# Nine more pairs of k tiles by seven products, in the convolution, merge and down blocks of a hybrid decoder layer

## The chip, the core and the metric

The kernel runs on one core of a Trainium2 chip. The metric is the device time of one execution in microseconds, as the median of several runs. TensorE (PE) multiplies, VectorE (DVE) and ScalarE (ACT) prepare its operands and take its results away, SyncE (SP) issues the transfers.

## What is computed

One layer on 256 tokens of width 2048, all in float32. Cut to what matters:

```python
h = rms_norm(x, mix_norm)
cb, cc, cx, q, k, v, g_conv, g_attn = split(h @ w_in)
conv_y = cb * causal_dwconv(cc * cx, conv_mix_w)
branch_conv = conv_y @ w_conv_out
branch_attn = dilated_window_attention(q, k, v) @ w_attn_out
merged = sigmoid(g_conv) * branch_conv + sigmoid(g_attn) * branch_attn
x = x + merged @ w_merge_out
g, u = split(causal_dwconv(rms_norm(x, ffn_norm) @ w_up, ffn_conv_w))
x = x + (silu(g) * u) @ w_down
```

## The kernel before

Every weight is read once, in chunks of 512 KB that SyncE loads into five `raw` buffers, and every chunk is split into a high and a low half: ScalarE rounds it (`whi`), VectorE subtracts (`wlo`, line 140). There are four buffers of each. The activations are held split in the same way, and a product is three matmuls: high by high, high by low, low by high.

The order is written out as a list of steps, one per chunk, and before each step's matmuls the program issues the loads up to eight chunks ahead and the splits up to three (`run_blocks`). A scheduler then puts each engine's instructions in a row, so their places need not be those of the code. Each engine works through its row in order.

The work runs through these blocks: cc, cx and cb (the three convolution inputs, in eight parts, 256 columns a chunk), then the convolution blocks gc, co, gc, co (the gate and the output of the convolution, 1024 columns each), q, k, v and ga (the attention, and its gate), ao (`W_ao`), mo (`W_mo`, the merge, four blocks of 512 columns), then twice eleven parts of ug and uv (the two halves of the up projection) and the down projection dn: two blocks of 1024 columns after the first eleven parts, one of 1024 and two of 512 after the second.

The 1024-column blocks are made by `block_h` and run by `run_h`. They take two k tiles (two chunks) at a time. An ordinary pair is eight products: two halves of tokens by two halves of columns by two tiles. A pair named in `PAIRS` or `DOWN_PAIRS` is a 2 x 2 product of blocks done with seven products on sums of the operands. For that, `split_sums` makes from the two chunks w11, w12, w22, w21 the sums `pq` and `rt` and splits four units, on VectorE:

```python
units = [split_unit(a[:, 1:2])]
nc.vector.tensor_tensor(pq[:, 0], w11, w12, op=ALU.add)
nc.vector.tensor_tensor(pq[:, 1], w12, w22, op=ALU.add)
units.append(split_unit(pq))
units.append(split_unit(b))
nc.vector.tensor_tensor(rt[:, 0], pq[:, 0], w22, op=ALU.add)
nc.vector.tensor_tensor(rt[:, 1], rt[:, 0], w21, op=ALU.add)
units.append(split_unit(rt))
```

A `split_unit` is one `whi` (line 147) and one `wlo` (line 148) and takes one of the four split buffers: the first has 512 columns, the others 1024. `make_forms` makes the four sums of activations that the seven products need, once for each pair. Four of the products gather over all such pairs of a block in `m1`, `m5`, `m6` and `m7` (`m16` holds the first and the third of them in one tile), and after the last such pair `combined` forms four sums of them on VectorE, which are added to the block's accumulators by its closing function.

A block's closing function, on VectorE: after cc, cx, cb, ug and uv a sum of two halves of the accumulator (`fsum`, ScalarE's copy `cba` or `upa` first), products with the norm, and for cx, ug and uv the convolution over three tokens (`dwconv`); after gc four sums; after co eight; after dn four.

Of the kernel before, what the change touches and what calls it, by code (L numbers as in the profile page):

```python
# [15 lines left out]
ALU = mybir.AluOpType  # L16
AX = mybir.AxisListType

P = 128
D = 2048  # L20
S = 256
NT = S // P
KT = D // P
# [7 lines left out]
CW = 512  # L31
# [15 lines left out]

K4_BUFS = 25
K2_BUFS = 16
PAIRS = (2, 4)  # L50
DOWN_PAIRS = (2, 5, 8)
RAW_BUFS = 5
WARM = 8
SPLIT_BUFS = 4
# [14 lines left out]
def hybrid_block(ctx: ExitStack, tc: tile.TileContext, x, x_turned, positions, gains, params, q_norm,  # L69
                 k_norm, w_first, w_rest, out):  # L70

    nc = tc.nc
# [9 lines left out]
    def k4(name, dtype=F32):  # L82
        return kpool.tile([P, 4 * S], dtype, tag="k4", name=name)

    def k2(name, dtype=F32):
        return kpool.tile([P, 2 * S], dtype, tag="k2", name=name, bufs=K2_BUFS)
# [81 lines left out]
    def after(n, fn):  # L168
        cur["n"] += 1
        side.append((cur["chunk"] + n, cur["n"], fn))  # L170
# [39 lines left out]
    def block_h(w, c0, r0, kts, src, forms, pairs, evac, name, **more):  # L210
        b = {"kts": kts, "mode": "H", "src": src, "forms": forms, "pairs": pairs, "evac": evac,
             "name": name, **more}
        blocks.append(b)
        for k in range(kts):
            if k // 2 in pairs:
                strassen[len(steps)] = None if k % 2 == 0 else k // 2
            steps.append((b, k, 1))
            chunks.append((w, r0 + k * P, 1, c0, 2 * CW))
# [68 lines left out]
    def make_forms(z, name, whole=True):  # L287
        t_ = k2(name + "f").rearrange("p (f s) -> p f s", f=4)
        if whole:
            both = k4(name + "F", F32R).rearrange("p (h f s) -> p h f s", h=2, f=4)  # L290
            hi, lo = both[:, 0], both[:, 1]
        else:
            hi, lo = (k2(name + "F", F32R).rearrange("p (f s) -> p f s", f=4) for _ in range(2))
        x11, x12, x21, x22 = (z[:, k, t * P:(t + 1) * P] for t in range(NT) for k in range(2))
        for n, a, b, op in ((0, x22, x21, ALU.subtract), (1, t_[:, 0], x11, ALU.add),
                            (2, x11, x21, ALU.subtract), (3, x12, t_[:, 1], ALU.subtract)):
            nc.vector.tensor_tensor(t_[:, n], a, b, op=op)
        nc.scalar.activation(hi, t_, AF.Copy)
        nc.vector.tensor_tensor(lo, t_, hi.bitcast(F32), op=ALU.subtract)
        return hi, lo  # L300
# [66 lines left out]
    def load_x(t_, c, cw, eng=nc.sync):  # L367
        v = t_.rearrange("p (t n) -> p t n", t=NT)
        eng.dma_start(v, x_v[:, :, c * cw:(c + 1) * cw])
        return v  # L370
# [16 lines left out]
    def row_squares(xs, ssq, c):  # L387
        junk = k2("junk")
        n = xs.shape[2]
        for t in range(NT):  # L390
            nc.scalar.activation(junk[:, :n], xs[:, t, :], AF.Square, accum_out=ssq[:, t, c:c + 1])
# [4 lines left out]
    def transposed(xs, i, gain0, store, name):  # L396
        store[i] = k4(name, F32R)
        pv = parts(store[i])
        tp_ = bank("tp")
        for k in range(2):  # L400
            for t in range(NT):
                done["tp"] = nc.tensor.transpose(tp_[:, k * S + t * P:k * S + (t + 1) * P],
                                                 xs[:, t, k * P:(k + 1) * P], ident)
        for k in range(2):
            g = cols[:, gain0 + 2 * i + k:gain0 + 2 * i + k + 1]
            src = tp_[:, k * S:(k + 1) * S]
            h = nc.scalar.activation(pv[:, k, 0, :], src, AF.Copy, scale=g)
            l = nc.vector.scalar_tensor_tensor(pv[:, k, 1, :], src, g, pv.bitcast(F32)[:, k, 0, :],
                                               op0=ALU.mult, op1=ALU.subtract)
        return h, l  # L410
# [93 lines left out]
    def ev_cb(nb):  # L504
        def evac(ps):
            z = fsum(ps, "cb")

            def gated():
                nc.vector.tensor_tensor(v2(z), v2(z), bc(rb1), op=ALU.mult)
                nc.vector.tensor_tensor(z, z, keep.pop("y"), op=ALU.mult)  # L510
                cy[nb] = split2(z, "conv")
                if nb in PAIRS:
                    cy_forms[nb] = make_forms(v2(z), "conv")
# [232 lines left out]
        return evac  # L746


    mg = [None] * 8

    def ev_attn_out(nb):
        def turned(half):
            i = 2 * nb + half
            mg[i] = k4("mg", F32R)
            pv = parts(mg[i])
            tp_ = bank("tp")
            for k in range(2):
                for t in range(NT):
                    c = (2 * half + k) * P
                    nc.tensor.transpose(tp_[:, k * S + t * P:k * S + (t + 1) * P],  # L760
                                        gattn[nb][t][:, c:c + P], ident)
            tv = tp_.rearrange("p (k s) -> p k s", k=2)
            nc.scalar.activation(pv[:, :, 0, :], tv, AF.Copy)
            nc.vector.tensor_tensor(pv[:, :, 1, :], tv, pv.bitcast(F32)[:, :, 0, :], op=ALU.subtract)

        def evac(ps):
            for t in range(NT):
                nc.vector.tensor_tensor(gattn[nb][t], ps[:, t, :], gattn[nb][t], op=ALU.mult)
                nc.vector.tensor_tensor(gattn[nb][t], gattn[nb][t], m1[nb][t], op=ALU.add)
            for half in range(2):  # L770
                after(1 + half, lambda half=half: turned(half))
        return evac

    x2, H2 = [None] * 4, [None] * 8
    ssq2 = cpool.tile([P, NT, 4], F32, name="ssq2")
    norm2 = {}

    def ev_merge(nb):
        def evac(ps):
            x2[nb] = load_x(k4("x2"), nb, CW)  # L780
            nc.vector.tensor_tensor(x2[nb], ps, x2[nb], op=ALU.add)
            for half in range(2):
                after(half, lambda half=half: transposed(x2[nb][:, :, half * 2 * P:(half + 1) * 2 * P],
                                                         2 * nb + half, 16, H2, "h2"))
            row_squares(x2[nb], ssq2, nb)
            if nb == 3:
                norm2["r"], norm2["rb"] = rms_rows(ssq2, "r2")
                after(3, lambda: rms_bcast(norm2["r"], norm2["rb"]))
        return evac
# [58 lines left out]
    W_in, W_co, W_ao, W_mo, W_up, W_dn = "w_in", "w_conv_out", "w_attn_out", "w_merge_out", "w_up", "w_down"  # L848
# [5 lines left out]
    for nb in range(2):  # L854
        block_h(W_in, COL_GC + nb * 2 * CW, 0, KT, x_src, x_forms, PAIRS, ev_gate_h(gconv, nb), "gc")
        block_h(W_co, nb * 2 * CW, 0, KT, cy_src, cy_forms, PAIRS, ev_conv_out_h(nb), "co")
    for half in range(2):
        for g in range(GROUPS):
            c = (g * SLOTS + half * 4) * HD
            block(W_in, COL_Q + c, 0, KT, "T", x_src, ev_qk(qT, gq, g, "q"), "q")  # L860
            block(W_in, COL_K + c, 0, KT, "T", x_src, ev_qk(kT, gk, g, "k"), "k")
        for g in range(GROUPS):
            c = (g * SLOTS + half * 4) * HD
# [7 lines left out]
    for nb in range(4):  # L871
        block(W_ao, nb * CW, 0, SLOTS, "T", at_src, ev_attn_out(nb), "ao")
    m_src = src_of(mg)
    for nb in range(4):
        block(W_mo, nb * CW, 0, KT, "T", m_src, ev_merge(nb), "mo")
    h_src = src_of(H2)
    for b0, b1 in ((0, NB // 2), (NB // 2, NB)):
# [46 lines left out]
    after(RB_AT, lambda: rms_bcast(r1, rb1))  # L924
    for n, i in enumerate(PAIRS):
        after(56 + 4 * n, behind(lambda i=i: forms_of_x(i)))
# [41 lines left out]
```

## Time and profile before

| what | value |
|---|---|
| median of 3 runs | 1846.84 us (1841.93 to 1851.29) |
| the profiled execution's own time | 1851.43 us |
| its span, first to last instruction | 1849.6 us |
| TensorE busy | 1843.5 us of the span |
| VectorE busy | 1279.6 us |
| ScalarE busy | 950.2 us |
| granted TensorE clock, mean | 1.000 |

The durations of matmuls overlap, so a sum of them is more than the time they take; the time from start to start is what each costs. The same holds to a smaller degree on VectorE: the next instruction can start before the one ahead is shown as ended.

### The profile page before, as it was taken

Reading aid. Unit: us, or ns where it says so; the run is one execution under the profiler, and the core shown is the slowest. Engines: PE = TensorE matmul, PEld = TensorE weight load, DVE = VectorE, ACT = ScalarE, POOL = GpSimd, SP = SyncE. Lnnn points to the kernel's source line nnn. Section 1 sums busy time; section 2 is a strip of 40 time slices with the busy share of each in tenths; the row PEclk is TensorE's granted clock in tenths of the full one; section 3 lists DMA queues with packets and bytes.
Section 4 is the critical chain, followed back from the end, with each engine's and each line's share of the span. In section 5 each row is a group of like instructions: output and inputs, shape, how many; then the busy total and the mean of one; then the engine's idle time right before and its main releaser. Section 6 shows DMA issues by size and latency. Waiting matters only on the chain.

```text
span 1849.6 us, 24483 instructions
## 1 busy us (share of the span) xinstructions
PE 1843.5 (100%) x9305; PEld 1561.4 (84%) x9305; DVE 1279.6 (69%) x1761; ACT 950.2 (51%) x1211; POOL 5.3 (0%) x18
## 2 busy tenths in 40 slices
PE   9999999999999999999999999999999999999999
PEld 8888888888888888888888888888888888888887
DVE  6787667777666474666566656777787867777774
ACT  6555445554555454554544455555554555555542
POOL 0000000000000000000000000000000000000000
PEclk9999999999999999999999999999999999999999
DMA  9555556566555535555535665555556665555563
GB/s 330 187 185 195 191 183 194 193 205 205 180 186 188 194 118 182 182 182 190 185 128 181 205 204 184 191 192 188 190 186 194 203 201 185 185 189 184 182 229 124
DMA packets 100213, 350.56 MB, mean 190 GB/s; under 512 B 11264, under 2 KB 11904, under 8 KB 100096
## 3 DMA queue, kind: packets, MB, share of 16 engines
q1 hardware_dynamic: 99664, 348.59, 57.1%
q8 instruction: 73, 1.20, 0.3%
q10 hardware_dynamic: 432, 0.41, 0.1%
q14 instruction: 44, 0.36, 0.1%
HBM read 346.86 MB, written 2.10 MB: 189 GB/s over the span
## 4 chain that ended last, share of the span: by engine, by line
PE 99%; DMA 0%; ACT 0%; DVE 0%; DVEq 0%; issue 0%; ACTq 0%
PE ps_ug L343 9%; PE ps_uv L343 9%; PE ps_uv L344 5%; PE ps_ug L344 5%; PE ps_cc L343 3%; PE ps_cx L343 3%; PE ps_cb L343 3%; PE ps_dn L235 3%; PE ps_dn L237 3%; PE ps_dn L236 3%; PE ps_k L350 2%; PE ps_q L350 2%; PE ps_v L350 2%; PE ps_k L348 2%; PE ps_q L348 2%; PE ps_k L349 2%
## 5 line engine op out<-in xcount | busy, mean ns | idle before, releaser
L140 DVE TENSOR_TENSOR wlo<-raw,whi 128x1024 fp32r<-128x1024 f32 (+1 forms) x622 | 748.5, 1209 | 436.0 <-ACT whi L139 432.9
L139 ACT ACTIVATE whi<-raw 128x1024 fp32r<-128x1024 f32 (+1 forms) x622 | 650.6, 1048 | 687.9 <-PE ps_ug L343 91.0
L343 PE MATMUL ps_ug<-h,whi 128*128 128x512 f32 x704 | 247.5, 395 | 0.0
L343 PE MATMUL ps_uv<-h,whi 128*128 128x512 f32 x704 | 247.4, 395 | 0.0
L344 PE MATMUL ps_ug<-h,wlo 128*128 128x256 f32 x704 | 197.7, 281 | 0.0
L344 PE MATMUL ps_uv<-h,wlo 128*128 128x256 f32 x704 | 197.4, 280 | 0.0
L343 PEld LDWEIGHTS ps_ug<-h,whi 128*128 128x128 f32 x704 | 132.0, 187 | 31.0
L343 PEld LDWEIGHTS ps_uv<-h,whi 128*128 128x128 f32 x704 | 132.0, 187 | 30.9
L344 PEld LDWEIGHTS ps_ug<-h,wlo 128*128 128x128 f32 x704 | 133.0, 189 | 0.1
L344 PEld LDWEIGHTS ps_uv<-h,wlo 128*128 128x128 f32 x704 | 133.0, 189 | 0.0
L343 PE MATMUL ps_cc<-xT,whi 128*128 128x512 f32 x256 | 92.3, 403 | 1.3 <-DVE xT L905 1.3
L343 PE MATMUL ps_cx<-xT,whi 128*128 128x512 f32 x256 | 91.8, 401 | 0.0
L237 PE MATMUL ps_dn<-whi,act 128*128 128x512 f32 x210 | 81.8, 389 | 0.0
L235 PE MATMUL ps_dn<-whi,act 128*128 128x512 f32 x210 | 81.8, 390 | 0.0
L236 PE MATMUL ps_dn<-wlo,act 128*128 128x512 f32 x210 | 81.7, 389 | 0.0
L343 PE MATMUL ps_cb<-xT,whi 128*128 128x512 f32 x224 | 79.4, 399 | 0.0
L348 PE MATMUL ps_k<-whi,xT 128*128 128x512 f32 x192 | 75.8, 395 | 0.0
L348 PE MATMUL ps_v<-whi,xT 128*128 128x512 f32 x192 | 75.7, 394 | 0.0
L348 PE MATMUL ps_q<-whi,xT 128*128 128x512 f32 x192 | 75.5, 393 | 0.0
L350 PE MATMUL ps_k<-whi,xT 128*128 128x512 f32 x192 | 75.0, 390 | 0.0
L350 PE MATMUL ps_q<-whi,xT 128*128 128x512 f32 x192 | 74.9, 390 | 0.0
L350 PE MATMUL ps_v<-whi,xT 128*128 128x512 f32 x192 | 74.9, 390 | 0.0
(320 smaller groups left out, 3480.2 us busy)
## 6 DMA issues: line engine op xcount, KB each, us to landing
raw<-in_w_rest SPq DMA_DIRECT2D x640, 512.0 KB, 3.4
x<-in_x SPq DMA_DIRECT2D x8, 512.0 KB, 6.8
raw<-in_w_first SPq DMA_DIRECT2D x15, 256.0 KB, 5.4
xt<-in_x_turned SPq DMA_DIRECT2D x8, 256.0 KB, 5.1
out<-x SPq DMA_DIRECT2D x7, 256.0 KB, 5.7
xz<-in_x_turned SPq DMA_DIRECT2D x2, 256.0 KB, 3.6
raw<-in_w_first ACTq DMA_DIRECT2D x1, 256.0 KB, 3.9
taps<-in_params SPq DMA_DIRECT2D x1, 156.0 KB, 5.2
```

Source lines behind the costliest of these rows:

```text
L139: last["act"] = nc.scalar.activation(hi, raw, AF.Copy)
L140: last["dve"] = nc.vector.tensor_tensor(lo, raw, hi.bitcast(F32), op=ALU.subtract)
L235: nc.tensor.matmul(dst, x[0], hi, start=first, stop=False)
L236: nc.tensor.matmul(dst, x[0], lo, start=False, stop=False)
L237: nc.tensor.matmul(dst, x[1], hi, start=False, stop=last)
L343: nc.tensor.matmul(pm, hi[:, j, w_], xs, start=first, stop=False)
L344: done["pe"] = nc.tensor.matmul(pm[:, :S], lo[:, j, w_], xs[:, :S], start=False, stop=last)
L348: nc.tensor.matmul(pm, sh, hi[:, j, :], start=first, stop=False)
L349: nc.tensor.matmul(pm, sh, lo[:, j, :], start=False, stop=False)
L350: nc.tensor.matmul(pm, sl, hi[:, j, :], start=False, stop=last)
```

## The change

`PAIRS` gets a third pair, and all its pairs move: 1, 3, 5 in place of 2, 4 of the eight. `DOWN_PAIRS` gets a fourth, 1, 3, 6, 8 in place of 2, 5, 8 of the eleven. The first two blocks of the merge become one 1024-column block in which pairs 3 and 5 take seven products; its forms are made as the gates are turned, its share of `x` is loaded then, and its sums are added to `x2` when the second pair is done. The rest of the merge stays as it is.

```diff
-PAIRS = (2, 4)
-DOWN_PAIRS = (2, 5, 8)
+PAIRS = (1, 3, 5)
+MERGE_PAIRS = (3, 5)
+DOWN_PAIRS = (1, 3, 6, 8)
...
-    mg = [None] * 8
+    mg, mg_forms = [None] * 8, {}
...
+            if i == MERGE_PAIRS[-1]:
+                for c in range(2):
+                    x2[c] = load_x(k4("x2"), c, CW)
+            if i in MERGE_PAIRS:
+                z = k2("mgz")
+                nc.scalar.copy(z, tp_)
+                mg_forms[i] = make_forms(z.rearrange("p (k s) -> p k s", k=2), "mg", False)
...
+    def merge_sums(sums):
+        for t in range(NT):
+            for c in range(2):
+                other, op = sums[t, c]
+                nc.vector.tensor_tensor(x2[c][:, t], x2[c][:, t], other, op=op)
+
+    def normed_rows(nb, wait):
+        for half in range(2):
+            after(wait + half, lambda half=half: transposed(x2[nb][:, :, half * 2 * P:(half + 1) * 2 * P],
+                                                            2 * nb + half, 16, H2, "h2"))
+        row_squares(x2[nb], ssq2, nb)
+
+    def ev_merge_h(ps, sums):
+        for t in range(NT):
+            for c in range(2):
+                nc.vector.tensor_tensor(x2[c][:, t], ps[t][:, c], x2[c][:, t], op=ALU.add)
+        for c in range(2):
+            normed_rows(c, 1 + 2 * c)
...
-            for half in range(2):
-                after(half, lambda half=half: transposed(x2[nb][:, :, half * 2 * P:(half + 1) * 2 * P],
-                                                         2 * nb + half, 16, H2, "h2"))
-            row_squares(x2[nb], ssq2, nb)
+            normed_rows(nb, 0)
...
-    for nb in range(4):
+    block_h(W_mo, 0, 0, KT, m_src, mg_forms, MERGE_PAIRS, ev_merge_h, "mo", early=merge_sums)
+    for nb in range(2, 4):
         block(W_mo, nb * CW, 0, KT, "T", m_src, ev_merge(nb), "mo")
```

With it the scheduler's rows change. Lines of the helpers are one higher in the changed kernel, those of `ev_up` more. Three places matter.

VectorE at the head of the first down block, before, from the first unit of the block's first seven-product pair (its pair 2) on; the sums `up` and the convolution of the last up tile stand directly ahead of these rows:

```order
L148 TENSOR_TENSOR wlo<-raw,whi 128x512
L801 TENSOR_TENSOR upc<-upc 128x512
L156 TENSOR_TENSOR pq<-raw 128x512
L157 TENSOR_TENSOR pq<-raw 128x512
L445 TENSOR_TENSOR act<-upc,act 128x2x256
L160 TENSOR_TENSOR rt<-pq,raw 128x512
L148 TENSOR_TENSOR wlo<-pq,whi 128x1024
L148 TENSOR_TENSOR wlo<-raw,whi 128x1024
L161 TENSOR_TENSOR rt<-rt,raw 128x512
L148 TENSOR_TENSOR wlo<-rt,whi 128x1024
```

The same place in the changed kernel, where the first such pair is the block's pair 1; its 512-column split stands ahead of `up`, four rows further up:

```order
L456 SCALAR_TENSOR_TENSOR upc<-up,taps,upc 128x254 x2
L825 TENSOR_TENSOR upc<-upc 128x512
L157 TENSOR_TENSOR pq<-raw 128x512
L158 TENSOR_TENSOR pq<-raw 128x512
L446 TENSOR_TENSOR act<-upc,act 128x2x256
L161 TENSOR_TENSOR rt<-pq,raw 128x512
L149 TENSOR_TENSOR wlo<-pq,whi 128x1024
L149 TENSOR_TENSOR wlo<-raw,whi 128x1024
L162 TENSOR_TENSOR rt<-rt,raw 128x512
L157 TENSOR_TENSOR pq<-raw 128x512
L158 TENSOR_TENSOR pq<-raw 128x512
L149 TENSOR_TENSOR wlo<-rt,whi 128x1024
```

The split of the first unit has gone ahead of the up tile's closing work, and two sums of the block's next such pair stand before the last split.

TensorE in that pair, before, from the seventh product's high half on (`m16` is the sixth product's sum, `whi_11711` and `wlo_11712` the split of `rt`):

```order
L237 MATMUL ps_dn_11657<-whi_11705,act_9965 128x512
L235 MATMUL m16_11751<-whi_11711,actF_9969 128x512
L235 MATMUL ps_dn_11658<-whi_11711,act_9965 128x512
L236 MATMUL m16_11751<-wlo_11712,actF_9969 128x512
L237 MATMUL m16_11751<-whi_11711,actF_9970 128x512
```

And in the changed kernel, from the pair's second product on (`whi_11800` is the split of `pq`, `whi_11804` that of `raw`, `whi_11810` that of `rt`, `whi_11840` the next pair's first chunk):

```order
L236 MATMUL m5_11851<-whi_11800,actF_9888 128x512
L236 MATMUL m7_11852<-whi_11800,actF_9888 128x512
L236 MATMUL ps_dn_11788<-whi_11804,actF_9888 128x512
L237 MATMUL m5_11851<-wlo_11801,actF_9888 128x512
...
L236 MATMUL m16_11850<-whi_11810,actF_9888 128x512
L236 MATMUL ps_dn_11789<-whi_11810,act_9884 128x512
L236 MATMUL ps_dn_11788<-whi_11840,act_10100 128x512
L237 MATMUL m16_11850<-wlo_11811,actF_9888 128x512
```

High-half matmuls have gone ahead of low-half ones, three at a time where it was two; eight more matmuls stand at the dots. The last down block, and less so the first and third convolution block, have the same pattern; all other pairs keep the plain order.

VectorE at the head of the first convolution block, in the changed kernel, from the first unit's split on (`cb` is the closing work of the block before):

```order
L149 TENSOR_TENSOR wlo<-raw,whi 128x512
L439 TENSOR_TENSOR cb<-ps_cb,cba 128x512
L510 TENSOR_TENSOR cb<-cb,r1b 128x512
L511 TENSOR_TENSOR cb<-cb,cy 128x512
L157 TENSOR_TENSOR pq<-raw 128x512
L158 TENSOR_TENSOR pq<-raw 128x512
L446 TENSOR_TENSOR conv<-cb,conv 128x2x256
L161 TENSOR_TENSOR rt<-pq,raw 128x512
L149 TENSOR_TENSOR wlo<-pq,whi 128x1024
```

Before, the same row of instructions belonged to pair 2, one pair later, with the 512-column split behind `conv`.

## Rows read from the trace of the kernel before

**Rows 1.** Busy time, share and instructions of each engine, from the page.

```profile
PE 1843.5 (100%) x9305; PEld 1561.4 (84%) x9305; DVE 1279.6 (69%) x1761; ACT 950.2 (51%) x1211; POOL 5.3 (0%) x18
```

**Rows 2.** Waits of TensorE: for whom, us in total, times, longest.

```profile
PE ps_cc L343 <- DVE xT L905: 1.3, 1, 1.3
PE warm L363 <- DVE ones L358: 1.1, 1, 1.1
```

**Rows 3.** Matmuls of the last block: duration min/median/max, first and last start.

```profile
L348 PE MATMUL ps_last<-whi,act x44: 389/389/389, 1815.7 to 1845.0; 128*128 128x512 f32 x44
```

**Rows 4.** Busy time by stretch, PE PEld DVE ACT POOL: second convolution, first down block.

```profile
322.40:364.60 42.20, 42.20 (x187) 34.91 (x186) 32.52 (x37) 22.77 (x25) 0.00 (x0) 1.00 0.61 202
1362.70:1421.00 58.30, 58.30 (x257) 47.68 (x256) 47.40 (x58) 30.01 (x33) 0.00 (x0) 1.00 0.57 188
```

**Rows 5.** Timeline, first down block's head: start, us, engine, what; its first matmul, VectorE.

```profile
1362.83 0.39 PE L235 MATMUL ps_dn<-whi,act 128*128 128x512 f32 x1
1365.14 0.68 DVE L438 TENSOR_TENSOR up<-ps_uv,upa 128x512 f32<-128x512 f32 x1
...
1369.92 0.68 DVE L156 TENSOR_TENSOR pq<-raw 128x512 f32<-128x512 f32 x1
1370.53 0.68 DVE L157 TENSOR_TENSOR pq<-raw 128x512 f32<-128x512 f32 x1
...
1376.55 1.23 DVE L148 TENSOR_TENSOR wlo<-rt,whi 128x1024 fp32r<-128x1024 f32 x1 [1.19 <-ACT whi L147]
1377.69 4.62 DVE L140 TENSOR_TENSOR wlo<-raw,whi 128x1024 fp32r<-128x1024 f32 x4
```

**Rows 6.** Groups by line and shape: busy, mean ns, then idle ahead and its releaser.

```profile
L148 DVE TENSOR_TENSOR wlo<-rt,whi 128x1024 fp32r<-128x1024 f32 x17 | 20.8, 1224 | 19.2 <-ACT whi L147 19.2
```

**Rows 7.** Timeline of TensorE's weight loads, the same pair.

```profile
1377.83 0.19 PEld L236 LDWEIGHTS m<-wlo,actF 128*128 128x128 f32 x1 [0.28 <-DVE wlo L148]
```

**Rows 8.** Timeline of ScalarE, the same head.

```profile
1362.91 1.06 ACT L139 ACTIVATE whi<-raw 128x1024 fp32r<-128x1024 f32 x1 [1.71 <-PE ps_uv L343]
1363.87 0.58 ACT L437 ACTIVATE upa<-ps_uv 128x512 f32<-128x512 f32 x1
...
1371.30 1.06 ACT L147 ACTIVATE whi<-pq 128x1024 fp32r<-128x1024 f32 x1 [0.29 <-DVE pq L157]
1372.27 1.04 ACT L147 ACTIVATE whi<-raw 128x1024 fp32r<-128x1024 f32 x1
1375.45 1.06 ACT L147 ACTIVATE whi<-rt 128x1024 fp32r<-128x1024 f32 x1 [2.14 <-DVE rt L161]
1376.42 1.04 ACT L139 ACTIVATE whi<-raw 128x1024 fp32r<-128x1024 f32 x1
```

**Rows 9.** Timeline of VectorE, first convolution block's head.

```profile
282.26 0.68 DVE L438 TENSOR_TENSOR cb<-ps_cb,cba 128x512 f32<-128x512 f32 x1
...
283.71 0.69 DVE L510 TENSOR_TENSOR cb<-cb,cy 128x512 f32<-128x512 f32 x1
```

**Rows 10.** Timeline, the merge's first block: its first matmul, the gates' last sums.

```profile
1026.52 0.39 PE L348 MATMUL ps_mo<-whi,mg 128*128 128x512 f32 x1
...
1027.93 1.28 DVE L769 TENSOR_TENSOR gate<-gate 128x512 f32<-128x512 f32 x2
```

**Rows 11.** The tile raw from 1355 to 1425 us: loads, issue to landing.

```profile
DMA to landing us min/median/max: 3.2/4.3/5.7
```

**Rows 12.** Timeline of TensorE at the kernel's start, high-half matmuls of successive pairs.

```profile
6.12 0.76 PE L343 MATMUL ps_cc<-xT,whi 128*128 128x512 f32 x1 [1.29 <-DVE xT L905]
...
8.42 0.63 PE L343 MATMUL ps_cc<-xT,whi 128*128 128x512 f32 x1
...
9.06 0.63 PE L343 MATMUL ps_cx<-xT,whi 128*128 128x512 f32 x1
...
10.25 0.39 PE L343 MATMUL ps_cx<-xT,whi 128*128 128x512 f32 x1
...
10.59 0.40 PE L343 MATMUL ps_cx<-xT,whi 128*128 128x512 f32 x1
```

## The prediction

> **What bounds the kernel now.** I read the page's busy times first: TensorE is busy all but 6 of 1849.6 us, VectorE two thirds [rows 1]. The waits of TensorE are two, 2.4 us in all, both at the start [rows 2]. So the time is a stream of matmuls, and a change counts by the matmuls it takes out and by the waits it puts in. Busy matmul times overlap, so a matmul's price is the distance between starts: 43 groups of three 512-column matmuls take 29.3 us, 0.227 us each [rows 3], where one alone is shown with 389 ns. The stages that change run at that pace: 186 matmuls x 0.227 = 42.2 us for the second convolution block and 255 x 0.227 = 57.9 us for the first down block, shown as 42.2 and 58.3 [rows 4]. There is no slack to win other than matmuls.
>
> Behind TensorE stands VectorE. It makes the low half of each weight chunk, and a seven-product pair costs it more than an ordinary one. It works one instruction at a time in order, and the distance between starts of queued ones is 0.60 us for 512 columns and 1.13 for 1024 (four of the latter in 4.62) [rows 5].
>
> **What the change takes out.** Nine pairs of k tiles go from eight products to seven: one in each of four convolution blocks, two in the merge, one in each of three down blocks. A product is three matmuls: 9 x 3 = 27, x 0.227 = **6.1 us**, all on the path. That the merge's first 1024 columns become one block changes no count beside that; its transposes stay.
>
> **What it adds on VectorE, on average.** A seven-product pair is five instructions of 512 and three of 1024 columns, 3.0 + 3.4 = 6.4 us, against 2 x 1.13 = 2.3 for an ordinary pair: 4.1 us more. The first down block has 47.4 us of it in 58.3, and would have 51.5 in 57.6; the second convolution block 32.5 of 42.2, and would have 36.6 in 41.5 [rows 4]. About 90%, so VectorE doesn't become the bound by its sum. The new forms (under 2 us each, in the cc/cx/cb and up stages, where VectorE has a third of its time free) and ScalarE's share (0.97 of a larger split a time) I cost at nothing: those stages wait for TensorE to free split buffers, and if that cover went, each of the new sets of forms could cost its 1 to 2 us once.
>
> **Where it adds waits: the first pair of a block.** What matters is when the last of a pair's four split units is ready. There are four split buffers, so the fourth unit can't be copied until TensorE has finished the pair before; in steady state VectorE idles about 1.1 us ahead of that split (19.2 us in 17) [rows 6], and it just fits. The change moves the first seven-product pair from the third pair of a block to the second (numbers 2 to 1), 24 x 0.227 = 5.4 us earlier, while VectorE is still busy with what the block before left. At the head of the first down block that is the convolution of the last up tile.
>
> I count from T, that block's first matmul (1362.83). Before, the chain on VectorE runs from the sum `up` (1365.14) to the end of the split of `rt` (1377.69), 12.55 us [rows 5], and the pair starts at T + 10.9; even so TensorE waited 0.28 us for it [rows 7]. After, `up` can start earlier: ScalarE's copy `upa` no longer stands behind a chunk's split, so it begins at T + 0.2, when the last matmul before T has ended, and `up` at T + 0.8. The 512-column split is done ahead, so the chain is 0.60 shorter; two more sums of the next pair come into the idle 1.19 ahead of the last split, at 1.20. With the distances of [rows 5] and ScalarE's of [rows 8], high halves are ready at T + 7.3 (pq), 8.4 (raw), 11.5 (rt) and 12.5 (the next pair's first chunk), low halves at 8.6, 9.7 and 12.7. TensorE, in the order of the changed kernel, does 27 matmuls to T + 6.1, waits 1.2 for pq, does two, waits 0.6 for raw, does ten to 10.65, waits 0.85 for rt, does two, waits 0.55 for the next chunk, does one and is at 12.7. It has done 42 matmuls, 9.5 us of work: **3.2 us lost**. The second half's down block has the same chain: another 3.2.
>
> At the head of the first convolution block the chain is shorter (`cb`, two products, one split; 282.26 to 283.71 and on [rows 9]). By the same steps, from `cb` at T + 0.8: pq high 5.1, raw high 6.1, rt high 9.2, next chunk 10.2. TensorE waits 0.4 and 0.55 at rt and the next chunk: **0.9 us**. At the third convolution block the chain is eight sums of 0.60 that may start earlier, because half of the accumulators are final twelve matmuls before the block's end: I take 0.3, between 0 and the 0.9 of the first. The second and fourth block have four sums there, the second down block four sums and an empty up chain: 0. In the merge the seven-product pairs are numbers 3 and 5, far from the head; its transposes come two together after ten matmuls, T + 2.3, and the gates they read were ready 2.7 us after such a block's start before [rows 10], and the eight sums into `x2` end close to the next block's start: 0.4, between 0 and 1.
>
> One more wait hangs in there. The two sums ahead of the last split read weights of the pair after; the later chunk can be loaded only when the first sums have let go of its buffer, T + 6.1, and a load lands after 3.2 to 5.7 us, 4.3 in the middle [rows 11], so at T + 10.4 against the 10.9 at which VectorE wants it. I take 0; a late landing adds up to 0.9 at each of the two down heads.
>
> Sum: -6.1 + 3.2 + 3.2 + 0.9 + 0.3 + 0.4 = **+1.9 us**. The profiled execution's own time is 1851.43 us, which would be 1853.3; it lies 4.6 above the median of the runs, 1846.84, and the same difference on that gives **1848.8 us**, 0.1% more.
>
> The price of an instruction on VectorE decides 6.4 of this. Rows show 0.68 us for one of 512 columns, but a new one every 0.60 [rows 5]. [...]
>
> **The rivals.** (1) The waits are hidden and all the matmuls are won: 1846.84 - 6.1 = 1840.7. For it: TensorE waited only 0.28 us at the same chain before, and its order is laid so that later matmuls fill waits. Against it: what fills is two or three high-half matmuls, 0.7 us. Chance 0.17.
> (2) Slower: the sums that close a block stand ahead of the next block's first split everywhere, and all seven heads with a pair number 1 cost what the down head costs: 7 x 3.2 = 22.4, less 6.1, plus 0.4, so +16.7: 1863.5. It decides from the point at which the backlog of VectorE at a head passes the 5.4 us that the ordinary pair gives. Against it: at those four heads the closing sums are 2.4 to 4.8 us and half of them can run before the block ends. Chance 0.11.
> (3) The clock. [...] Chance 0.04.
> That the change doesn't do what it says can be left aside: 27 matmuls are gone from the order.
>
> **How the numbers follow.** The forecast has 0.68. Its own bounds: waits at the heads of 4 (1.6 us each at the down heads, 0.8 elsewhere) to 12 us (late loads and the queue's longer price at both, 0.9 and 1 for the small ones) give 1844.7 to 1852.7. The range reaches down to rival 1 and up to half of rival 2: **1841 to 1857**. A measurement of this kernel can tell about 0.5% (9.2 us) from no change. Faster by more than that can't come out of the sum, whose best is 0.33%: 0.03. Slower by more is rival 2 and a scatter of the runs: 0.12. Same: 0.85.
>
> **What would show it.** The trace after should have 27 matmuls fewer; new waits of TensorE at four places alone, the second pair of the first and third convolution block and of the first and last down block, 3 us in sum at each down head, for ScalarE's `whi<-pq` and `whi<-rt`; no longer block elsewhere. [...]

## The result, and the profile after

The changed kernel took 1851.99 us (median of 20 runs, 1845.32 to 1856.85), the kernel before 1846.74 us (20 runs, 1841.51 to 1851.29): a ratio of 1.0031, 95% interval 1.0019 to 1.0042. That is 3.5 to 7.8 us more, a loss inside the 0.5% that had been called the same. The profiled execution took 1856.62 us (its span 1854.8) against 1851.43 before. In all lists of the changed kernel line numbers are one higher than before.

The busy line, which answers to [rows 1]:

```profile
PE 1842.4 (99%) x9278; PEld 1554.8 (84%) x9278; DVE 1330.2 (72%) x1855; ACT 969.2 (52%) x1240; POOL 5.3 (0%) x18
```

TensorE has 27 matmuls fewer and still a longer span: there must be waits. These are all waits of TensorE in its list of waits (for whom, us in total, times, longest); [rows 2] had the two at the start alone:

```profile
PE m L236 <- ACT whi L148: 3.5, 5, 1.3
PE ps_cc L344 <- ACT whi L140: 1.3, 1, 1.3
PE warm L364 <- DVE ones L359: 1.0, 1, 1.0
PE m L237 <- DVE wlo L149: 0.7, 1, 0.7
PE ps_dn L236 <- ACT whi L148: 0.4, 2, 0.2
PE ps_dn L236 <- ACT whi L140: 0.4, 2, 0.2
PE ps_gc L236 <- ACT whi L140: 0.4, 2, 0.2
PE ps_co L237 <- DVE wlo L149: 0.4, 1, 0.4
PE ps_cx L345 <- DVE wlo L141: 0.2, 1, 0.2
```

The names say where: `m` and `ps_dn` with `whi` of L148 and L140 are the high halves of a seven-product pair and of the chunk behind it; `wlo` of L149 are low halves. The list gives 5.8 us for the new waits of the changed blocks, but a wait costs more than is listed, since the next matmuls also start late (0.31 to 0.35 us behind the one ahead at the head below, against 0.227). So I measured stages, from the first matmul of one to the first of the next, in every profile of the study. "ao" is the stage ahead of the merge; "down 1" is the two down blocks of the first half, "down 2" those of the second half up to `ps_last`. The stages not shown (attention 531.3 to 531.5, first half of the up projection 245.6) were the same in all to 0.2 us.

```
                 conv    ao  merge  down 1  down 2   cc/cx/cb  up, 2nd half
before         169.04 46.31  90.70  116.02   88.15     273.78        248.73
after          170.23 46.36  89.57  117.89   90.67     274.30        248.74
after_again    168.75 46.33  89.58  117.82   90.70     273.23        248.73
late           171.76 46.30  89.61  116.71   87.52     268.47        244.05
down_only      169.20 46.35  90.73  117.91   90.68     273.44        244.06
conv_only      170.54 46.32  90.67  116.02   88.19     268.86        248.73
merge_only     168.96 46.32  89.55  116.04   88.17     273.21        244.07
raw6           168.83 48.09  89.57  117.90   90.71     273.20        248.74
short_chain    168.47 46.33  89.59  115.64   88.50     273.91        248.73
late_raw6      172.77 48.12  89.57  115.96   87.53     268.77        244.07
best           171.18 48.11  89.60  115.49   88.54     273.50        244.07
conv14         170.10 46.30  89.57  116.02   88.15     273.83        248.73
best2          169.16 46.31  89.58  116.09   87.51     273.09        248.73
```

The matmuls taken out are worth 4 x 0.68 = 2.7 us in conv, 1.4 in the merge, 1.4 in down 1 and 0.7 in down 2 (0.227 each, [rows 3]). After minus before: conv +1.2, merge -1.1, down 1 +1.9, down 2 +2.5. So 3.9, 0.2, 3.2 and 3.2 us were lost, to waits and to the late starts behind them.

The head of the first down block, TensorE's timeline (start, us, engine, what, in brackets the wait). The pace is a matmul every 0.227 us ([rows 3]); what is longer is a wait or a late start:

```profile
1363.44 0.39 PE L236 MATMUL ps_dn<-whi,act 128*128 128x512 f32 x1
...
1369.38 0.39 PE L238 MATMUL m<-whi,act 128*128 128x512 f32 x1
1371.01 0.73 PE L236 MATMUL m<-whi,actF 128*128 128x512 f32 x2 [1.25 <-ACT whi L148]
1371.96 0.50 PE L236 MATMUL ps_dn<-whi,actF 128*128 128x512 f32 x1 [0.22 <-ACT whi L148]
...
1373.98 0.39 PE L236 MATMUL ps_dn<-whi,act 128*128 128x512 f32 x1
1374.21 0.40 PE L237 MATMUL ps_dn<-wlo,act 128*128 128x512 f32 x1
1374.44 0.40 PE L238 MATMUL ps_dn<-whi,act 128*128 128x512 f32 x1
1375.16 0.51 PE L236 MATMUL m<-whi,actF 128*128 128x512 f32 x1 [0.32 <-ACT whi L148]
1375.51 0.39 PE L236 MATMUL ps_dn<-whi,act 128*128 128x512 f32 x1
1376.11 0.50 PE L236 MATMUL ps_dn<-whi,act 128*128 128x512 f32 x1 [0.22 <-ACT whi L140]
```

What it waited for, on VectorE and on ScalarE, which answers to [rows 5, 8]:

```profile
1364.28 0.69 DVE L439 TENSOR_TENSOR up<-ps_uv,upa 128x512 f32<-128x512 f32 x1 [2.16 <-ACT upa L438]
...
1368.59 0.69 DVE L157 TENSOR_TENSOR pq<-raw 128x512 f32<-128x512 f32 x1
1369.19 0.68 DVE L158 TENSOR_TENSOR pq<-raw 128x512 f32<-128x512 f32 x1
...
1373.27 0.69 DVE L162 TENSOR_TENSOR rt<-rt,raw 128x512 f32<-128x512 f32 x1
1373.87 0.68 DVE L157 TENSOR_TENSOR pq<-raw 128x512 f32<-128x512 f32 x1
1374.47 0.69 DVE L158 TENSOR_TENSOR pq<-raw 128x512 f32<-128x512 f32 x1
1375.14 1.23 DVE L149 TENSOR_TENSOR wlo<-rt,whi 128x1024 fp32r<-128x1024 f32 x1
```

```profile
1369.90 1.06 ACT L148 ACTIVATE whi<-pq 128x1024 fp32r<-128x1024 f32 x1 [0.51 <-DVE pq L158]
1370.87 1.04 ACT L148 ACTIVATE whi<-raw 128x1024 fp32r<-128x1024 f32 x1
1374.05 1.06 ACT L148 ACTIVATE whi<-rt 128x1024 fp32r<-128x1024 f32 x1 [2.14 <-DVE rt L162]
```

With T = 1363.44: `up` at T + 0.8, and the high halves end at T + 7.5 (pq), 8.5 (raw) and 11.7 (rt). TensorE starts behind each within 0.05 us. The row at 1371.01 merges two matmuls; in a timeline that starts later the second stands by itself:

```profile
1371.35 0.40 PE L236 MATMUL m<-whi,actF 128*128 128x512 f32 x1
```

So the four gaps, less 0.227 each, are 1.40, 0.38, 0.49 and 0.37, 2.65 us together. Eight more matmuls at this head start 0.31 to 0.35 us behind the one ahead, without a listed wait: another 0.85. Before, this head had 0.25 us of such late starts, so the loss is 3.2.

### The profile page after: what moved, and what is told of

The parts are those of the page before. It is cut to its first block, busy times and chain, and to the rows that moved or that the text cites. A ratio compares the mean times of both kernels' runs of the same rounds, so it can differ in the third digit from the quotient of the medians.

```text
span 1854.8 us, 24561 instructions
## 1 busy us (share of the span) xinstructions
PE 1842.4 (99%) x9278; PEld 1554.8 (84%) x9278; DVE 1330.2 (72%) x1855; ACT 969.2 (52%) x1240; POOL 5.3 (0%) x18
## 4 chain that ended last, share of the span: by engine, by line
PE 96%; DVE 2%; DMA 2%; ACT 1%; issue 0%; ACTq 0%; DVEq 0%
PE ps_ug L344 9%; PE ps_uv L344 9%; PE ps_uv L345 5%; PE ps_ug L345 5%; PE ps_cx L344 3%; PE ps_cc L344 3%; PE ps_cb L344 3%; PE ps_k L351 2%; PE ps_v L351 2%; PE ps_q L351 2%; PE ps_k L349 2%; PE ps_q L349 2%; PE ps_k L350 2%; PE ps_v L349 2%; PE ps_v L350 2%; PE ps_q L350 2%
## 5 line engine op out<-in xcount | busy, mean ns | idle before, releaser
L141 DVE TENSOR_TENSOR wlo<-raw,whi 128x1024 fp32r<-128x1024 f32 (+1 forms) x604 | 726.2, 1209 | 387.0 <-ACT whi L140 383.7
L140 ACT ACTIVATE whi<-raw 128x1024 fp32r<-128x1024 f32 (+1 forms) x604 | 631.4, 1048 | 633.6 <-PE ps_ug L344 89.9
L236 PE MATMUL ps_dn<-whi,act 128*128 128x512 f32 x192 | 74.9, 390 | 0.4 <-ACT whi L140 0.4
L350 PE MATMUL ps_k<-wlo,xT 128*128 128x512 f32 x192 | 74.8, 390 | 0.0
L350 PE MATMUL ps_q<-wlo,xT 128*128 128x512 f32 x192 | 74.8, 389 | 0.0
```

The costliest lines, as they stand in the source:

```text
L140: last["act"] = nc.scalar.activation(hi, raw, AF.Copy)
L141: last["dve"] = nc.vector.tensor_tensor(lo, raw, hi.bitcast(F32), op=ALU.subtract)
L236: nc.tensor.matmul(dst, x[0], hi, start=first, stop=False)
L350: nc.tensor.matmul(pm, sh, lo[:, j, :], start=False, stop=False)
```

## The experiments

**Where the loss is: one part at a time.** Three kernels take one part of the change each.

Down blocks alone (kernel before):

```diff
-DOWN_PAIRS = (2, 5, 8)
+DOWN_PAIRS = (1, 3, 6, 8)
```

> The kernel before with DOWN_PAIRS (1, 3, 6, 8) alone: 9 matmuls fewer. Heads: 2.0 us won, 3.7 lost at each of the two blocks that follow an up tile, 0 at the second down block, so +5.3 us, ratio 1.0029. A loss of 1.26 us per added pair: +1.7 us, ratio 1.0009.

Measured: 1850.8 us, ratio 1.0025 (1.0004 to 1.0045). Down 1 took 117.91 and down 2 90.68, as in the changed kernel to 0.02 us. The losses of 3.2 us at each of the two heads belong to this part alone; 3.7 had been expected. In the two down stages the kernel is 4.4 us above the one before, nearer the 5.3 of the heads than the 1.7 of a price per pair.

Convolution blocks alone (kernel before):

```diff
-PAIRS = (2, 4)
+PAIRS = (1, 3, 5)
```

> The kernel before with PAIRS (1, 3, 5) alone: 12 matmuls fewer, 2.7 us. Heads and a late load, as in the trace of the change: 1.5 lost in the first, 0.1 in the second, 0.6 in the third and 1.9 in the fourth block, so +1.4 us, ratio 1.0008. A loss of 1.26 us per added pair: +2.3 us, ratio 1.0013.

Measured: 1847.51 us, ratio 1.001 (0.999 to 1.003). Its conv stage took 170.54, so 4.2 us were lost, more than the 2.7 won. Over the pace its four blocks lost 1.6, 0.9, 0.3 and 1.5 us; in the second 0.1 had been expected.

The merge alone (changed kernel, with the other two tables set back):

```diff
-PAIRS = (1, 3, 5)
+PAIRS = (2, 4)
-DOWN_PAIRS = (1, 3, 6, 8)
+DOWN_PAIRS = (2, 5, 8)
```

> The kernel before with the merge's new block alone (pairs 3 and 5), PAIRS (2, 4), DOWN_PAIRS (2, 5, 8): 6 matmuls fewer. Heads: no head is touched, 1.4 us won, ratio 0.9993. A loss of 1.26 us per added pair: +1.2 us, ratio 1.0006.

Measured: 1845.58 us, ratio 1.0004 (0.9987 to 1.0021). The merge stage took 89.55, 1.15 less than before. The interval holds both expectations, 0.9993 and 1.0006; the stage decides for the first. Of the three parts this is the one that pays.

**Is it the first pair's place? All pairs one later** (changed kernel):

```diff
-PAIRS = (1, 3, 5)
+PAIRS = (2, 4, 6)
-DOWN_PAIRS = (1, 3, 6, 8)
+DOWN_PAIRS = (2, 4, 6, 8)
```

> The changed kernel with the same number of seven-product pairs, but none in a block's second place: PAIRS (2, 4, 6), DOWN_PAIRS (2, 4, 6, 8), the merge as changed. 27 matmuls fewer than before. If the loss sits at the heads of the blocks, where pair number 1 finds VectorE still busy: no wait over 0.5 us at any head, 6.1 us less than before, ratio to before 0.997, about 1841. If each added seven-product pair costs its share of VectorE wherever it stands (11.3 us lost over nine pairs, 1.26 each): as slow as the change, ratio 1.003.

Measured: 1849.14 us, ratio 1.0016 (0.9998 to 1.0033). Where the last pair is far from the block's end, the place was it: down 2 took 87.52, all of its 0.7 us won and nothing lost. But conv took 171.76 (5.4 us lost) and down 1 116.71 (2.0 lost). The waits of TensorE in this kernel that are not in [rows 2]:

```profile
PE m L237 <- DVE wlo L149: 2.0, 4, 0.9
PE ps_co L236 <- DVE gate L536: 1.2, 2, 0.6
...
PE ps_gc L236 <- DVE m L545: 0.6, 1, 0.6
PE ps_q L349 <- DVE m L545: 0.6, 1, 0.6
```

Lines 536 and 545 are the sums that close a convolution block. With the last seven-product pair at number 6 of 0 to 7 they come so late that the next block's first matmul waits for their PSUM banks. At the second block's start:

```profile
316.70 0.39 PE L238 MATMUL ps_gc<-whi,xT 128*128 128x512 f32 x1
317.69 0.47 PE L236 MATMUL ps_co<-whi,conv 128*128 128x512 f32 x1 [0.60 <-DVE gate L536]
```

The gap is 0.99, with 0.31 behind it: 0.85 us lost, at each of the four block ends, 3.4 in all. The remainder, in conv and in the first half's second down block, are waits for a low half `wlo` of L149, behind sums that waited for a load. So the pair's place at the head is one cause among several; the theory that it is the only one fell.

**Is it what stands ahead of the sums?** In this kernel the convolution of the last value tile of each half of the up projection is left out (that part of the computation is missing in it), which takes four instructions of VectorE and two of ScalarE out of the queue at the down heads:

```diff
-            y = dwconv(u, lambda k, f: fconv[:, k, c + f:c + f + 1], "upc")
+            y = u if is_val and b % (NB // 2) == NB // 2 - 1 else dwconv(u, lambda k, f: fconv[:, k, c + f:c + f + 1], "upc")
```

> The changed kernel with the depthwise convolution left out for the last value tile of each half of the up projection (part of the computation is left out there): four VectorE and two ScalarE instructions fewer between the last up tile and the sums of the first seven-product pair of the following down block. Theory, queue ahead of the sums: the sums start some 3 us sooner (the first at about 3.6 instead of 6.6 us behind that tile's last matmul), the four waits at each of the two down heads go from 3.7 us together to 0 to 0.8, so the stage of the first two down blocks goes from 117.9 to 114.7 to 115.2 us and the second half's from 90.7 to 87.5 to 88.0. Rival, the pair itself: its own 6.4 us of VectorE work against 4.8 us of matmuls makes the waits, whatever stands ahead: 117.9 and 90.7 stay within 0.5 us.

Measured: down 1 115.64 and down 2 88.50, 2.25 and 2.2 us less than in the changed kernel; its one run took 1850.05 us. The same rows of VectorE, with T = 1361.24:

```profile
1362.07 0.69 DVE L439 TENSOR_TENSOR up<-ps_uv,upa 128x512 f32<-128x512 f32 x1 [2.16 <-ACT upa L438]
...
1364.13 0.68 DVE L157 TENSOR_TENSOR pq<-raw 128x512 f32<-128x512 f32 x1
...
1367.69 1.22 DVE L149 TENSOR_TENSOR wlo<-raw,whi 128x1024 fp32r<-128x1024 f32 x1
1368.82 0.68 DVE L162 TENSOR_TENSOR rt<-rt,raw 128x512 f32<-128x512 f32 x1
```

and the waits of TensorE that are left there:

```profile
PE m L236 <- ACT whi L148: 0.3, 1, 0.3
PE ps_dn L236 <- ACT whi L140: 0.2, 1, 0.2
```

The first sum is at T + 2.9 instead of T + 5.15, and as much time comes back; half a us more had been expected. What stays is the gaps for rt and for the next chunk, 0.50 and 0.38 over the pace, as long as with the full queue (0.49 and 0.37). A shorter queue does not touch them. In the rows the second sum of rt stands behind the low halves of pq and raw, so I put this 1 us down to the pair itself; the queue was shortened, not emptied, and this was not tried by itself.

**Is it the same at a convolution head?** The merge-only kernel, with one of the two convolution pairs moved to the head:

```diff
-PAIRS = (2, 4)
+PAIRS = (1, 4)
```

> The kernel with the merge part of the change alone, with the convolution blocks' two pairs at 1 and 4 instead of 2 and 4: as many seven-product pairs as before, one moved to the head. Theory, the head costs: the first and third blocks wait as in the changed kernel (1.5 and 0.65 us over the pace), conv stage 169.0 + 2.1 = 171.1 us. Rival, three pairs in eight are too many for VectorE and the loads, and their place does not matter: conv 169.0 us.

Measured: conv 170.10, against 168.96 to 169.20 in the four kernels with pairs 2 and 4; 1851.51 us in its one run. Behind the start, TensorE's waits are at the first block's head alone, the same two as in the changed kernel:

```profile
288.70 0.39 PE L238 MATMUL ps_gc<-whi,xT 128*128 128x512 f32 x1
289.41 0.50 PE L236 MATMUL m<-whi,xF 128*128 128x512 f32 x1 [0.32 <-ACT whi L148]
...
290.36 0.49 PE L236 MATMUL ps_gc<-whi,xT 128*128 128x512 f32 x1 [0.21 <-ACT whi L140]
```

The place costs the first head 1.0 us net. The third block does not wait here. In the changed kernel it waited 0.21 us at its head in one execution and showed no listed wait there in the next (below), so one profile without it says little. Both the theory and the rival were half right.

**The fourth convolution block and the loads.** Here the prediction had 0, and the trace of the changed kernel shows 2.0 us over the pace. TensorE loses most of it in the block's second seven-product pair (number 3): its low halves stand on VectorE behind the first sum of the third such pair (number 5), and that sum waited. Of VectorE and of TensorE:

```profile
424.06 0.69 DVE L157 TENSOR_TENSOR pq<-raw 128x512 f32<-128x512 f32 x1 [3.82 <-DMA raw<-in_w_rest]
```

```profile
425.94 0.50 PE L237 MATMUL ps_co<-wlo,convF 128*128 128x512 f32 x1 [0.35 <-DVE wlo L149]
...
428.28 0.50 PE L237 MATMUL m<-wlo,convF 128*128 128x512 f32 x1 [0.68 <-DVE wlo L149]
```

The load that the sum waited for had been issued at 418.45, one of three within 1.8 us (417.32, 418.45, 419.06), when VectorE let go of three buffers in a row, with the low halves of the ordinary pair and the first split of the next. The three were in flight together, and this one landed 5.6 us after its issue. VectorE ran its row in order: the sum started at 424.06 and the two low halves behind it at 424.67 and 427.01, so they were late as well. The burst by itself need not cost anything: in the kernel before three loads of this block were issued within 1.8 us too (421.79, 422.93, 423.53) and landed after 3.3, 5.0 and 5.7 us, and TensorE did not wait. No later seven-product pair follows there whose sum could stand in front of low halves.

A second execution of the same kernel:

> The changed kernel once more, to see what a second profiled execution keeps. Theory, waits set by the order of the instructions: the two down stages give 117.9 and 90.7 us again and the first and third convolution blocks wait again at their first pair, all within 0.1 us. What came from a load that landed late (the fourth convolution block's wait of 1.9 us in all) may come out between 0.5 and 1.9 us, so the conv stage between 168.5 and 170.3 us. Rival, all waits are alike from run to run: conv 170.2 within 0.2 us.

Measured: 1853.95 us; down 117.82 and 90.70 again, and 1.4 us over the pace in the first convolution block again. The third block lost 0.3 instead of 0.6 us and its head is no longer in the list of waits, so the theory failed there. Conv took 168.75, 1.5 us less, most of it in the fourth block, where the load landed 4.6 us after its issue instead of 5.6 and the same sum waited 2.9 us instead of 3.82:

```profile
DVE pq L157 <- DMA raw<-in_w_rest: 2.9, 1, 2.9
```

Four profiled executions have the convolution blocks of the changed kernel: 170.23, 168.75, 170.54 (convolution alone) and 168.47 (the shortened chain). In this order the sum waited 3.8, 2.9, 3.6 and 2.8 us, and the fourth block lost 2.0, 0.9, 1.5 and 0.6 us over the pace: the loss follows the wait. The kernels with pairs 2 and 4 and five raw buffers lie within 0.24 of each other. So this wait hangs on when loads land, and costs 0.6 to 2 us. The 0.9 us of the second block in the kernel with the convolution pairs alone are the same wait for a low half.

A sixth raw buffer, with two `k2` buffers fewer to make room:

```diff
-K2_BUFS = 16
+K2_BUFS = 14
-RAW_BUFS = 5
+RAW_BUFS = 6
```

> The changed kernel with a sixth raw buffer (and two k2 buffers fewer, to make room). In the changed kernel the fourth convolution block lost 1.9 us, most of it in its third pair, where VectorE's first sum waited 3.82 us for a raw load that was issued only when a buffer had come free. Theory, late buffer: with one more buffer that load is issued earlier, the wait goes, and the conv stage (first gc matmul to first q matmul) falls from 170.23 us to 168.3 to 168.7; the two down stages, whose heads wait for the sums' chain and not for a load, stay at 117.9 and 90.7 us; the median is 1.5 to 2 us lower than the changed kernel's. Rival, VectorE too full there: the waits stay whatever is loaded, conv 170.2. Rival, the transfers themselves are too slow: the load lands as late as before, conv 170 or more.

Measured: 1853.61 us, ratio 1.0025 (1.0004 to 1.0046) to the kernel before. A median 1.5 to 2 us below the changed kernel's had been expected; the ratios, 1.0025 and 1.0031, cannot tell that. Conv took 168.83, near the 168.3 to 168.7 that were expected, but that decides nothing, since it lies among the four executions above, and a sum of the same pair still waited:

```profile
421.28 0.69 DVE L158 TENSOR_TENSOR pq<-raw 128x512 f32<-128x512 f32 x1 [2.30 <-DMA raw<-in_w_rest]
```

The burst of three comes 1 us earlier in the block, and its second load still took 5.3 us to land; the wait moves from the first sum to the second. And a new wait came in, 1.8 us in the ao stage, in all three kernels with these buffer counts:

```profile
PE ps_ao L349 <- DVE gate L776: 1.5, 1, 1.5
```

Which of the two counts brings it was not tried.

The later pairs with the same buffers:

> The late pairs (2, 4, 6 and 2, 4, 6, 8) with a sixth raw buffer. With five buffers its conv stage took 171.76 us: 0.76 to 0.85 us lost at each of the four block ends, where the next block's first matmul waited for VectorE's closing sums to free its PSUM banks, and some 2 us in the middle of blocks, where sums waited for loads; its first down stage took 116.7 us, 2 us over the sum of its matmuls, behind sums that waited for loads. Theory: the waits in the middle go, those at the block ends stay: conv 169.7 to 170.3, first down stage 114.7 to 115.2, second 87.5. Rival, VectorE too full: conv 171.8 and down 116.7 stay.

Measured: 1851.23 us, ratio 1.0008 (0.9984 to 1.0033). Down 1 fell from 116.71 to 115.96, half of what was expected; conv rose to 172.77, because the gaps at three block ends grew from 0.99 to 1.43. With these two counts more raw buffers are no cure.

**A version that keeps what pays.** First with six raw buffers, pairs (2, 4), the merge as changed, and (2, 4, 6, 8) in the down blocks:

> Two pairs (2, 4) in the convolution blocks as before, the merge's two pairs as changed, four pairs (2, 4, 6, 8) in the down blocks, and a sixth raw buffer: the parts whose stages were seen to win. Theory: conv 169.0 us as before, the merge stage 89.55 (1.1 less than before), the first down stage 114.7 to 115.2 (0.8 to 1.3 less), the second 87.5 (0.65 less): 2.6 to 3.1 us less than the kernel before, a median near 1844 and a ratio of 0.9985. Rival, the sixth buffer takes nothing off: first down stage 116.7, about 1 us less in all.

Measured: 1848.04 us, ratio 0.9996 (0.9975 to 1.0018). Conv 171.18 and ao 48.11 gave the gain away, and down 1 (115.49) and down 2 (88.54) came out above the expected 115.2 and 87.5. Four kernels with the same convolution pairs and the old buffer counts had 168.96 to 169.20 in conv, so I put its rise down to the counts; there is one profile of it. Then with five buffers, and four pairs in the second half's down block alone (merge-only kernel):

```diff
-DOWN_PAIRS = (2, 5, 8)
+DOWN_PAIRS = ((2, 5, 8), (2, 4, 6, 8))
...
-                if b % (NB // 2) in DOWN_PAIRS:
+                if b % (NB // 2) in DOWN_PAIRS[b // (NB // 2)]:
...
-            block_h(W_dn, 2 * nb * CW, b0 * FW, 2 * (b1 - b0), a_src, act_forms, DOWN_PAIRS,
+            block_h(W_dn, 2 * nb * CW, b0 * FW, 2 * (b1 - b0), a_src, act_forms, DOWN_PAIRS[b0 // (NB // 2)],
```

> The parts whose stages won, with five raw buffers: two pairs (2, 4) in the convolution blocks, the merge's two pairs, three pairs (2, 5, 8) in the first half's down blocks and four (2, 4, 6, 8) in the second half's. Theory: conv 169.0, merge stage 89.55 (1.1 less than before), first down stage 116.0, second 87.5 (0.65 less): 1.8 us less than the kernel before in its stages, a ratio near 0.999, which five rounds can hardly tell from 1. Rival, the second half's block waits for loads as the first half's second block did with these pairs: 88.5 us there, 0.8 us less than before in all.

Measured: ratio 0.9986 (0.9966 to 1.0006) to the kernel before; 1849.52 us beside 1851.14 in the same session. Its stages came out as expected (89.58 and 87.51), 1.8 us less in merge and down 2, and TensorE waits only at the start again, in the first 21 us; this is its whole list:

```profile
PE ps_cc L344 <- ACT whi L140: 1.3, 1, 1.3
PE warm L364 <- DVE ones L359: 1.0, 1, 1.0
PE ps_cc L345 <- DVE wlo L141: 0.5, 2, 0.2
PE ps_cx L345 <- DVE wlo L141: 0.2, 1, 0.2
```

Its interval lies below the changed kernel's (1.0019 to 1.0042), so it is better than that one; against the kernel before its gain is seen in the stages, not in the interval.

## Why the prediction was right, and where it was off

Forecast was 1848.8 us, +1.9, in a range of 1841 to 1857, with 0.85 for the same. It came out at 1851.99, +5.2.

**The matmuls taken out** (-6.1): right; 9305 - 27 = 9278 are left, and they come every 0.227 us between waits.

**The two down heads** (3.2 each): right in place and in cause, and in size partly by luck. The chain was counted to end its high halves at T + 7.3, 8.4 and 11.5, and did at 7.5, 8.5 and 11.7. The waits were counted as 1.2, 0.6, 0.85 and 0.55, 3.2 in all, and came as 1.40, 0.38, 0.49 and 0.37, 2.65 in all. The late starts of the matmuls around them, 0.6 us more than before, had no term; the two errors cancel, and the stages lost 3.2 and 3.2. (The 0.28 us of [rows 7] is such a case: it is idle time of the weight load, and the matmul there and the one behind it started 0.02 and 0.10 us late.) The two sums of the next pair filled VectorE's idle time ahead of the split of rt, as said (1373.87 and 1374.47). No load was late there. Leaving out part of that chain gave 2.2 us of each back, and with the pair one place later down 2 lost nothing, so the cause is shown and not only counted; how the last 1 us of it comes about is read from the rows.

**The price on VectorE**: the queue's 0.60 us for 512 columns was right (1368.59 to 1369.19), and 1024 columns came 1.13 to 1.15 apart (1370.99, 1372.14, 1373.27). The forecast's upper bound of 12 us also counted a longer price in the queue; no run shows that term. At this head a sum of 512 columns is shown with 0.68 to 0.69 us, and the next one starts after 0.60.

**The merge** (0.4): 0.2.

**The convolution blocks** (0.9 at the first, 0.3 at the third, 0 at the second and fourth): this is the term that was mis-sized. The stage lost 3.9 us in the profiled execution, 2.1 to 4.2 over four, where 1.2 stood. At the first head the two forecast waits (0.4 and 0.55) came as 0.49 and 0.37, 0.9 as forecast, but late starts, which had no term here either, made it 1.4 over the pace. The third block lost 0.6 in this execution, and the forecast 0.3 in the next one and in two more kernels with these pairs. The larger part of the excess is the fourth block. There the closing sums at the head were looked at and found short, which was right to 0.35 us, and the loads were not. A load that lands late for the next pair's sum was weighed at the down heads alone, where it stayed at 0, and not at the later pairs of the convolution blocks, where such a sum stands ahead of two low halves as well. [Rows 11] had the landing times, up to 5.7 us, and the load in question took 5.6. So new waits came at a fifth place, where the prediction named four alone.

With the measured terms the sum is -6.1 + 3.2 + 3.2 + 0.2 + (2.1 to 4.2) = +2.6 to +4.7 us. The two profiled executions of the changed kernel were 5.2 and 2.5 us above the profiled one of before. The measured 3.5 to 7.8 reaches higher than this sum. The runs of both kernels lie in groups (last section). By eye, group against group, the changed kernel is some 4 us higher: the lowest runs are 1841.51 and 1845.32, and the middle of the next group is 1846.6 and 1850.5. That lies in the sum. The medians lie further apart, 5.2, and 5 of the 20 runs before fell into the lowest group but only 2 after; that the change causes this mix is not shown.

**The rivals.** Waits hidden: refuted, they are in the list. All seven heads at the full price: refuted, three of them lose 0 to 0.35 and two 0.6 and 1.4. The clock: the one or two matmuls directly behind a wait come 0.31 to 0.35 apart, but from then on they come 0.23 apart (1373.98, 1374.21, 1374.44). At the kernel's start, in the trace of before, pairs of matmuls came 0.64 us apart and then 0.34 [rows 12], with a granted clock of 1.00 in that stretch too; the same ratio would be some 0.41 to 0.43 here, as an estimate from these distances. It is not seen behind the new waits, of which the longest was 1.3 us, and the granted clock at the first down head is 1.00. What slowed the start is not shown.

## What to carry to other kernels

Here, taking matmuls out of a stream that waits for nothing paid where the engine that prepares their operands had slack at that very place (1.1 us less in the merge), and not where it had none (3.2 us lost at each of two down heads). An average of 86% (VectorE is shown busy 101.89 of the 117.89 us of down 1) hides both a head, where the queue still holds the last block's work, and a tail, where closing sums hold the PSUM banks (0.85 us lost at each convolution block's end with the later pairs). Count the chain at the head instruction by instruction in starts, not durations; here that gave the times of the high halves to 0.2 us. Give the late starts behind a wait a term too, about 0.1 us each here. And for every pair whose sums move ahead in the row, ask when its loads land and what stands behind the sums: here loads issued within 2 us of each other landed up to 6.3 us later, and two low halves waited with the sum.

## What the runs showed of the hardware

Two stages run at one of two steady paces in an execution, without waits that would explain it, and with a granted clock of 1.00 in the two stretches below. In the second half of the up projection, the group of `ps_ug` matmuls of the changed kernel and of the kernel with the later pairs (duration min/median/max, first and last start):

```profile
L344 PE MATMUL ps_ug<-h,whi x351: 387/398/404, 1481.7 to 1718.4; 128*128 128x512 f32 x176
```

```profile
L344 PE MATMUL ps_ug<-h,whi x352: 391/394/396, 1476.0 to 1708.6; 128*128 128x512 f32 x176
```

The same matmuls take 236.7 or 232.6 us: a pair of 512 and 256 columns every 0.3533 or 0.3467 us (the stage, 248.73 or 244.05 us, over its 704 pairs). The cc/cx/cb stage does the same, independently (273 to 274 or 268 to 269 us in the table). Every mixture of the two occurs in the table. No kernel was profiled at both paces; that the pace changes between executions of one kernel is read from its run times, which lie in groups some 4.7 us apart (1841.4 to 1842.7, 1846.3 to 1847.3, 1850.1 to 1852.3 in 35 runs of the kernel before). Both paces together move an execution by up to 10 us, twice the effect studied. Later sessions have a fourth group (1855.1 to 1857.4) that these two stages do not reach. This is why the stage table, and not the medians, carries the reading above. What sets the pace is not known.
